# Sums of squares over all channels from a rounded pair instead of one float32 product, at three norms of a hybrid encoder layer

## Chip, core and metric

The kernel runs on one core of a Trainium2 chip. The metric is the device time of one execution in microseconds; the median of several runs counts. TensorE is called PE, VectorE DVE, ScalarE ACT, GpSimd POOL and SyncE SP, as in the profile.

## The reference

One streaming step of one layer, for 512 prompt frames and 64 sample frames (576 columns in the kernel), with 2048 channels:

```python
def rmsnorm(x, g):
    xf = x.astype(jnp.float32)
    y = xf * lax.rsqrt(jnp.mean(xf * xf, axis=-1, keepdims=True) + EPS) * g.astype(jnp.float32)
    return y.astype(x.dtype)

def hybrid_layer(x, ...):
    hn = rmsnorm(x, g_norm1)
    proj = hn @ w_in
    ...
    o_attn = stick_breaking_blocks(q, k_all, v_all, P).reshape(B, T, ATTN_W)
    ...
    o_conv = gb * conv
    mix = jnp.concatenate([rmsnorm(o_attn, g_attn_out), rmsnorm(o_conv, g_conv_out)], axis=-1)
    x = x + mix @ w_out
    h2 = rmsnorm(x, g_norm2)
    x = x + (jax.nn.silu(h2 @ w_gate) * (h2 @ w_up)) @ w_down
```

Four of its norms take a mean of squares over many channels. The change touches three: the one of the convolution's output (1024 channels), the one of the attention's output (1024) and the second norm of the layer (2048, `g_norm2`). The first norm of the layer and the norms of each head's queries and keys are as they were.

## The kernel before

**Layout.** Channels lie on the 128 partitions, frames on the free axis, in two halves of 288 columns (`HALVES`). Matmuls are done in rounded float32 (`F32R`), and each float32 operand is parted into a rounded part `hi` (a cast on ACT, L228) and the rest `lo` (a subtraction on DVE, L229), by `split`. A product is then three matmuls: hi*hi, lo*hi, hi*lo.

**Stages.** First the input projection, in units of weights (`HEADS_A`), each as seven products (`run`, `multiply`, L405) of sums of blocks of weights and inputs. Then the output projection in two passes (`out_proj`, L224): over the convolution's channels (`mixc`), with the attention of the eight heads running between its products, and over the attention's channels (`mixa`). Then the gate, up and down products of the feed-forward part, again as seven products per unit. Weights come by DMA to `raw_a` and `raw_b` (L328); sums of weight blocks are formed on DVE (L345, L349, L351, L353, with `s` a sum of blocks), and `prepare` parts a piece of weights into `whl` (128 x 1024, L228 and L229) four products ahead of its use. `psy`, `psx`, `psw` and `psv` are the PSUM banks of these products; `part` is a copy of psy (L428).

**The three norms.** The squares of the channels are added up elementwise as they are made: `accc` for the convolution, `accA` for the attention (both 128 x 576), `acc2` (two tiles of 128 x 288) for the second norm. What is left is the sum over the 128 partitions, which a matmul with a matrix of ones (`oner`) does and at once spreads to all partitions. In `group_scale` and `row_scale2` this is one plain float32 product per half (L866, L1416) into the bank `ssg` or `ss2`; then ACT and DVE form the inverse root: a scaled copy (L869, L1418), logarithm (L870, L1419), exponential (L871, L1420), square (L872, L1421), and two operations on DVE (L873 and L874, L1422 and L1423). The result stands in `accc` or `accA`, which scales the products of `out_proj` (L1110), or in `R2`, which scales the gate and up products (L1512). The norms of the heads (`normed`) already sum by `channel_sums`: two rounded matmuls (L283, L284) of parted squares; their parts `s2` are made by `a_done`, 12 to 24 ticks ahead.

**What sets the order.** PE's instructions run in the order in which the program is written. Work beside the products is in generators of a `Pipeline`: every group of three matmuls is a tick, and `yield n` puts a generator off by n ticks. `group_scale(accc[0], 3)` is spawned 13 ticks after a product of the input projection's last but one unit, `group_scale(accA, 2)` 9 ticks ahead of the second pass's place for it, and `row_scale2` waits 19 ticks into the feed-forward part. On ACT, DVE, POOL and SP a scheduler sets the order when the program is built; on the chip each engine then executes its queue in that order, and an instruction that waits holds what is behind it. Buffers of the pool `tmp` with the tag `hl` (128 x 2 x 288) go round between all users of the tag, three of them in the first stages and two from the second pass on.

The Silu of the gate (L1517) and the logarithm and exponential are in different function tables of ACT; a change between them is an `ACT_TABLE_LOAD`.

Of the kernel before, what the change touches and what calls it, by code (L numbers as in the profile page):

```python
# [10 lines left out]
F32 = mybir.dt.float32  # L11
F32R = mybir.dt.float32r
# [4 lines left out]
P = 128  # L17
# [3 lines left out]
HALF = T // 2  # L21
# [81 lines left out]
def tile_hybrid_stream_step(  # L103
# [7 lines left out]
    mm = nc.tensor.matmul  # L111
# [13 lines left out]
    tmp = tc.alloc_tile_pool(name="tmpa", bufs=2, side="left")  # L125
# [15 lines left out]
    def misc(name):  # L141
        return ps_z.tile([P, 512], F32, tag="misc", name=name, bufs=2)
# [75 lines left out]
    pipe = Pipeline()  # L218
# [8 lines left out]
    def split(hi, lo, src, lo_eng=None):  # L227
        cast = nc.scalar.copy(out=hi, in_=src)  # L228
        (lo_eng or nc.vector).tensor_tensor(out=lo, in0=src, in1=hi.bitcast(F32), op=ALU.subtract)  # L229
        return cast.ins  # L230
# [8 lines left out]
    oner = const.tile([P, P], F32R, name="oner")  # L239
# [41 lines left out]
    def channel_sums(src_hi, src_lo, a, b, name):  # L281
        ps = misc(name)[:, : b - a]
        mm(ps, oner, src_hi, start=True, stop=False)  # L283
        mm(ps, oner, src_lo, start=False, stop=True)  # L284
        return ps
# [576 lines left out]

    def group_scale(acc_, bufs):
        for a, b in HALVES:
            ss = misc("ssg")[:, :HALF]
            mm(ss, oner.bitcast(F32), acc_[:, a:b], start=True, stop=True)  # L866
            yt = tmp.tile([P, 2, HALF], F32, tag="hl", name="ytg", bufs=bufs)
            y, t = yt[:, 0], yt[:, 1]
            nc.scalar.activation(out=ss, in_=ss, func=AF.Identity, scale=1.0 / (8 * P), bias=epsc)  # L869
            nc.scalar.activation(out=y, in_=ss, func=AF.Ln)  # L870
            nc.scalar.activation(out=y, in_=y, func=AF.Exp, scale=-0.5)  # L871
            nc.scalar.activation(out=t, in_=y, func=AF.Square)  # L872
            nc.vector.scalar_tensor_tensor(out=t, in0=t, scalar=-0.5, in1=ss, op0=ALU.mult, op1=ALU.mult)  # L873
            nc.vector.scalar_tensor_tensor(out=acc_[:, a:b], in0=t, scalar=1.5, in1=y, op0=ALU.add, op1=ALU.mult)  # L874
            yield 1
# [118 lines left out]
    for k_, (n, p_) in enumerate(order):  # L994
        run(n, p_, n in early)
        if k_ + 4 < len(order):
            prepare(*order[k_ + 4])
            if order[k_ + 4] in ((-2, 3), (-1, 6)):
                load_weight()
        if (n, p_) == (-2, 6):  # L1000
            pipe.spawn(group_scale(accc[0], 3), 13)
        if (n, p_) == (-1, 3):
            xpool.release()
            cpool = tc.alloc_tile_pool(name="cpool", bufs=1, reuse_waits="tile", side="right")
            mixc = cpool.tile([P, NG, 2, T], F32R, name="mixc")
            for g in range(NG):
                nc.sync.dma_start(out=mixc[:, g].bitcast(F32), in_=mixc_dram[g])
        if (n, p_) == (-1, 5):
            split_weight(nc.vector)
        if (n, p_) == (-1, 7):  # L1010
            first = next_weight(), ps_pj.tile([P, HALF], F32, tag="pj", name="pjo")
            product(first[1], *first[0], slice(0, P), mixed_conv, 8, 0, HALF)
# [307 lines left out]
    accA = bt["accA"]  # L1320
# [3 lines left out]
    tmp = tc.alloc_tile_pool(name="tmp", bufs=2, reuse_waits="tile", side="left")  # L1324
    lpad = tc.alloc_tile_pool(name="lpad", bufs=1, side="left")
    lpad.tile([P, 64], F32, name="lpad_t")
    pipe.spawn(group_scale(accA, 2), 9)

# [14 lines left out]
    acc2 = [apool.tile([P, HALF], F32, name=f"acc2_{i}") for i in range(2)]  # L1345
# [66 lines left out]
    def row_scale2():  # L1412
        yield 19
        for i, (a, b) in enumerate(HALVES):
            ss = misc("ss2")[:, :HALF]
            mm(ss, oner.bitcast(F32), acc2[i], start=True, stop=True)  # L1416
            y, t = (tmp.tile([P, HALF], F32, tag=tag, name="y2") for tag in ("y", "r"))
            nc.scalar.activation(out=ss, in_=ss, func=AF.Identity, scale=1.0 / D, bias=epsc)  # L1418
            nc.scalar.activation(out=y, in_=ss, func=AF.Ln)  # L1419
            nc.scalar.activation(out=y, in_=y, func=AF.Exp, scale=-0.5)  # L1420
            nc.scalar.activation(out=t, in_=y, func=AF.Square)  # L1421
            nc.vector.scalar_tensor_tensor(out=t, in0=t, scalar=-0.5, in1=ss, op0=ALU.mult, op1=ALU.mult)  # L1422
            nc.vector.scalar_tensor_tensor(out=R2[:, a:b], in0=t, scalar=1.5, in1=y, op0=ALU.add, op1=ALU.mult)  # L1423
        apool.release()

    pipe.spawn(row_scale2())
    tpool.release()

# [311 lines left out]
```

## Time and profile before

| | |
|---|---|
| median of 3 runs | 2326.66 us (2326.58 to 2326.91) |
| the profiled execution: time | 2327.18 us |
| its span in the profile | 2325.5 us |
| PE busy | 2315.3 us |
| DVE, ACT, POOL busy | 1951.5, 1222.1, 304.3 us |
| sums of accc, accA, acc2 on PE | at 538.6, 752.6 and 859.7 us |

Times in views are microseconds from the span's start. In rows of the timeline stand the start, the duration, the engine, the line, the operation, output<-inputs, the shape, and the number of instructions taken together; in brackets the idle time of the engine ahead of it and what ended that. PE's matmuls are pipelined: one of 288 columns has a duration of 0.29 us, while the next starts 0.13 us after it. PEld is the load of a stationary operand, beside the matmuls. The Ls are line numbers of the kernel before.

### The profile page before, as it was taken

How to read it: one execution, taken by the hardware profiler on the slowest of the kernel's cores; microseconds unless marked ns; L12 is line 12 of the kernel's file. 1: busy time of each engine (PE TensorE's matmuls, PEld its weight loads, DVE VectorE, ACT ScalarE, POOL GpSimd, SP SyncE). 2: the span in 40 equal slices, each digit the busy share in tenths (PEclk: the TensorE clock that was granted, in tenths of full speed). 3: DMA queues.
4: the chain of work that ended last, by engine and by line, in shares of the span. 5: the costliest groups of instructions: out<-in, count | busy, mean ns of one | idle time of the engine just before them, and what ended most of it. 6: DMA issues, size and time to landing. Idle time of an engine off the chain costs nothing.

```text
span 2325.5 us, 43556 instructions
## 1 busy us (share of the span) xinstructions
PE 2315.3 (100%) x17432; PEld 2306.9 (99%) x17432; DVE 1951.5 (84%) x2871; ACT 1222.1 (53%) x2170; POOL 304.3 (13%) x374
## 2 busy tenths in 40 slices
PE   9999999999999999999999999999999999999999
PEld 9999999999999999999999999999999999999999
DVE  8898989897777898888888888888888777987897
ACT  8566656456887564444444444444444444444443
POOL 0212121110432320000000000000000002431222
PEclk9999999999999999999999999999999999999999
DMA  8444343546653554544444444344344936885654
GB/s 273 136 118 130 91 142 107 147 129 209 191 148 101 173 200 128 155 138 141 149 135 150 131 148 155 112 157 157 117 155 134 351 129 205 228 240 184 209 128 108
DMA packets 533674, 368.57 MB, mean 158 GB/s; under 512 B 70246, under 2 KB 517888, under 8 KB 533472
## 3 DMA queue, kind: packets, MB, share of 16 engines
q1 hardware_dynamic: 526976, 356.42, 48.8%
q0 software_dynamic: 6384, 9.24, 2.3%
q8 instruction: 136, 2.23, 0.4%
q14 instruction: 66, 0.54, 0.1%
q10 hardware_dynamic: 112, 0.14, 0.0%
HBM read 285.52 MB, written 80.23 MB: 157 GB/s over the span
## 4 chain that ended last, share of the span: by engine, by line
PE 94%; ACT 3%; DVE 2%; POOL 1%; issue 0%; DMA 0%; SPq 0%; POOLq 0%; ACTq 0%; DVEq 0%
PE psy L405 47%; PE psw L405 24%; PE psx L405 12%; PE pjo L224 6%; PE pj L691 1%; PE pjz L691 1%; PE psv L405 1%; PE pjm L691 1%; ACT ph L228 0%; PE psx L556 0%; DVE pr L1134 0%; DVE wlo L177 0%; POOL pr L1189 0%; ACT whi L176 0%; DMA vtok<-v_dram 0%
## 5 line engine op out<-in xcount | busy, mean ns | idle before, releaser
L229 DVE TENSOR_TENSOR whl<-raw_a,whl 128x1024 fp32r<-128x1024 f32 (+4 forms) x384 | 429.8, 1120 | 55.5 <-ACT whl L228 54.1
L405 PE MATMUL psy<-t,whl 128*128 128x288 f32 x3000 | 447.0, 294 | 0.0
L228 ACT CAST whl<-raw_a 128x1024 fp32r<-128x1024 f32 (+4 forms) x384 | 360.1, 940 | 140.0 <-PE psx L405 44.9
L405 PE MATMUL psy<-h_s,whl 128*128 128x288 f32 x2766 | 416.6, 294 | 0.0
L405 PEld LDWEIGHTS psy<-t,whl 128*128 128x128 f32 x3000 | 414.4, 188 | 0.0
L405 PE MATMUL psw<-t,whl 128*128 128x288 f32 x2688 | 388.9, 294 | 0.0
L405 PEld LDWEIGHTS psy<-h_s,whl 128*128 128x128 f32 x2766 | 383.1, 188 | 0.2
L405 PEld LDWEIGHTS psw<-t,whl 128*128 128x128 f32 x2688 | 366.8, 188 | 0.0
L228 ACT CAST whl<-raw_b 128x1024 fp32r<-128x1024 f32 (+5 forms) x234 | 211.4, 905 | 208.2 <-issue 71.4
L229 DVE TENSOR_TENSOR whl<-raw_b,whl 128x1024 fp32r<-128x1024 f32 (+5 forms) x234 | 256.1, 1095 | 73.4 <-ACT whl L228 72.4
L428 ACT COPY part<-psy 128x288 f32<-128x288 f32 x309 | 123.2, 399 | 347.9 <-PE psy L405 345.5
L405 PE MATMUL psx<-h_s,whl 128*128 128x288 f32 x1164 | 170.2, 294 | 0.0
L228 ACT CAST whl<-s 128x1024 fp32r<-128x1024 f32 (+5 forms) x103 | 95.3, 925 | 124.3 <-PE psw L405 116.4
L405 PEld LDWEIGHTS psx<-h_s,whl 128*128 128x128 f32 x1164 | 159.6, 188 | 0.0
L405 PE MATMUL psw<-t34a,whl 128*128 128x288 f32 x1056 | 150.4, 295 | 0.0
L405 PE MATMUL psy<-t12a,whl 128*128 128x288 f32 x1056 | 150.4, 295 | 0.0
L405 PEld LDWEIGHTS psw<-t34a,whl 128*128 128x128 f32 x1056 | 143.5, 188 | 0.0
L405 PEld LDWEIGHTS psy<-t12a,whl 128*128 128x128 f32 x1056 | 143.3, 188 | 0.2
L1455 POOL DMA_DIRECT2D hid_dram<-form x7 | 5.2, 736 | 951.6 <-DVE form L229 944.5
L229 DVE TENSOR_TENSOR whl<-s,whl 128x1024 fp32r<-128x1024 f32 (+5 forms) x103 | 110.3, 1071 | 20.3 <-ACT whl L228 19.6
L224 PE MATMUL pjo<-mixc,whi 128*128 128x288 f32 x512 | 118.7, 299 | 0.0
L224 PE MATMUL pjo<-mixa,whi 128*128 128x288 f32 x512 | 102.8, 295 | 0.0
(565 smaller groups left out, 3922.0 us busy)
## 6 DMA issues: line engine op xcount, KB each, us to landing
hid_dram<-form SPq DMA_DIRECT2D x147, 288.0 KB
raw_a<-in_w_in_dram SPq DMA_DIRECT2D x22, 1024.0 KB
raw_b<-in_w_in_dram SPq DMA_DIRECT2D x22, 1024.0 KB
raw_b<-in_w_gate_dram SPq DMA_DIRECT2D x22, 1024.0 KB
raw_b<-in_w_up_dram SPq DMA_DIRECT2D x22, 1024.0 KB
raw_a<-in_w_gate_dram SPq DMA_DIRECT2D x22, 1024.0 KB
raw_a<-in_w_up_dram SPq DMA_DIRECT2D x22, 1024.0 KB
h_s<-hid_dram SPq DMA_DIRECT2D x10, 2016.0 KB
```

Source lines behind the costliest of these rows:

```text
L224: mm(ps, w_[:, k, csl], x_[:, a:b], start=(k == 0 and n == 0), stop=(k == nk - 1 and n == 2))
L228: cast = nc.scalar.copy(out=hi, in_=src)
L229: (lo_eng or nc.vector).tensor_tensor(out=lo, in0=src, in1=hi.bitcast(F32), op=ALU.subtract)
L405: mm(ps, whl[:, w_, j, :], x_, start=(start and j == 0 and q == 0), stop=(j == len(xs_) - 1 and q == 2), skip_group_check=True)
L428: nc.scalar.copy(out=t, in_=st["y"])
L691: mm(banks_[c][i], w3[:, kt % 8, c * P : (c + 1) * P], t[:, x_, :], start=(kt == 0 and n == 0), stop=(kt == KD - 1 and n == 2))
L1455: q.dma_start(out=hid_dram[fp][2 * n - 2 : 2 * n].rearrange("f p t -> p f t"), in_=t.bitcast(F32))
```

## The change

At all three norms each half of the sum of squares is first parted by `split` into a new tile (`s2g`, `s2r`), with a cast on ACT and a subtraction on DVE. Three ticks later (two in `row_scale2`) `channel_sums`, which was there for the heads, multiplies both parts by the ones, as two rounded matmuls into one bank. In `group_scale` the second half's split comes only after the first half's sums; the spawn for `accA` is three ticks earlier in exchange.

```diff
     def group_scale(acc_, bufs):
         for a, b in HALVES:
-            ss = misc("ssg")[:, :HALF]
-            mm(ss, oner.bitcast(F32), acc_[:, a:b], start=True, stop=True)
+            s2 = tmp.tile([P, 2, HALF], F32R, tag="hl", name="s2g", bufs=bufs)
+            split(s2[:, 0], s2[:, 1], acc_[:, a:b])
+            yield 3
+            ss = channel_sums(s2[:, 0], s2[:, 1], a, b, "ssg")
             yt = tmp.tile([P, 2, HALF], F32, tag="hl", name="ytg", bufs=bufs)
...
-    pipe.spawn(group_scale(accA, 2), 9)
+    pipe.spawn(group_scale(accA, 2), 6)
...
     def row_scale2():
         yield 19
         for i, (a, b) in enumerate(HALVES):
-            ss = misc("ss2")[:, :HALF]
-            mm(ss, oner.bitcast(F32), acc2[i], start=True, stop=True)
+            s2 = tmp.tile([P, 2, HALF], F32R, tag="hl", name="s2r", bufs=2)
+            split(s2[:, 0], s2[:, 1], acc2[i])
+            yield 2
+            ss = channel_sums(s2[:, 0], s2[:, 1], a, b, "ss2")
```

What it calls, unchanged:

```python
    def split(hi, lo, src, lo_eng=None):
        cast = nc.scalar.copy(out=hi, in_=src)
        (lo_eng or nc.vector).tensor_tensor(out=lo, in0=src, in1=hi.bitcast(F32), op=ALU.subtract)
        return cast.ins

    def channel_sums(src_hi, src_lo, a, b, name):
        ps = misc(name)[:, : b - a]
        mm(ps, oner, src_hi, start=True, stop=False)
        mm(ps, oner, src_lo, start=False, stop=True)
        return ps
```

In the changed kernel the lines behind the first edit have numbers two higher (L871 is L869 of before), those behind the last four higher. On PE, POOL and SP the rest of the order is the same, but for two neighbouring DMAs on SP that change places. On PE the sums stand later: at place 1 (accc) the first pair comes three groups of three psy matmuls later, at the end of that product, and the second after twelve matmuls of the following psx product; at place 2 (accA) the first pair has the slot of the first float32 product, the second comes 12 matmuls behind it, where before there were three; at place 3 (acc2) the first pair comes after 18 matmuls of a psy product instead of 12, the second six matmuls later, where before both products stood together.

Place 1, DVE's queue at the convolution's norm, before (`yt` and `E` belong to a head's norm, `ytg` to this one):

```order
L353 TENSOR_TENSOR raw_a<-raw_a 128x8x128
L853 SCALAR_TENSOR_TENSOR yt<-yt,ss 128x288
L854 SCALAR_TENSOR_TENSOR yt<-yt 128x288
L855 SCALAR_TENSOR_TENSOR E_6158<-E_6158,gqs,yt 128x288
L229 TENSOR_TENSOR whl<-raw_a,whl 128x1024
L873 SCALAR_TENSOR_TENSOR ytg<-ytg,ssg 128x288
L874 SCALAR_TENSOR_TENSOR accc<-ytg 128x288
L229 TENSOR_TENSOR whl<-raw_b,whl 128x1024
L873 SCALAR_TENSOR_TENSOR ytg<-ytg,ssg 128x288
```

and now:

```order
L353 TENSOR_TENSOR raw_a<-raw_a 128x8x128
L229 TENSOR_TENSOR s2g<-accc,s2g 128x288
L853 SCALAR_TENSOR_TENSOR yt<-yt,ss 128x288
L854 SCALAR_TENSOR_TENSOR yt<-yt 128x288
L229 TENSOR_TENSOR whl<-raw_a,whl 128x1024
L855 SCALAR_TENSOR_TENSOR E_6158<-E_6158,gqs,yt 128x288
L229 TENSOR_TENSOR whl<-raw_b,whl 128x1024
L229 TENSOR_TENSOR s2g<-accc,s2g 128x288
L875 SCALAR_TENSOR_TENSOR ytg<-ytg,ssg 128x288
L876 SCALAR_TENSOR_TENSOR accc<-ytg 128x288
```

The first subtraction stands behind L353, the second behind the parting of a piece of raw_b. On ACT the second cast stands, in this order, behind a copy of psy (L428), the scaled copy of the first half (L869 of before), the cast of that piece of raw_b, and the first half's logarithm (L870).

Place 2, DVE's queue at the attention's norm, before (`wlo` are parts of the output projection's weights, `s` a sum of the first feed-forward weights):

```order
L177 TENSOR_TENSOR wlo_8787<-raw_a,whi_8786 128x512 x4
L345 TENSOR_TENSOR s_10011<-raw_b 128x1024
L873 SCALAR_TENSOR_TENSOR ytg<-ytg,ssg 128x288
L874 SCALAR_TENSOR_TENSOR accA<-ytg 128x288
L1110 TENSOR_TENSOR pjo<-pjo,accA 128x288
```

and now:

```order
L177 TENSOR_TENSOR wlo_8795<-raw_a,whi_8794 128x512 x2
L229 TENSOR_TENSOR s2g<-accA,s2g 128x288
L177 TENSOR_TENSOR wlo_8795<-raw_a,whi_8794 128x512 x2
L345 TENSOR_TENSOR s_10027<-raw_b 128x1024
L875 SCALAR_TENSOR_TENSOR ytg<-ytg,ssg 128x288
L229 TENSOR_TENSOR s2g<-accA,s2g 128x288
L876 SCALAR_TENSOR_TENSOR accA<-ytg 128x288
L1112 TENSOR_TENSOR pjo<-pjo,accA 128x288
```

The first subtraction stands amid the four wlo, the second behind the sum of raw_b (L345) and the first half's own L873.

Place 3, DVE's queue at the second norm, before (`t12z` and `t_7` are parts of the last input blocks):

```order
L229 TENSOR_TENSOR whl<-raw_a,whl 128x1024
L229 TENSOR_TENSOR t12z<-ta,t12z 128x288 x2
L229 TENSOR_TENSOR whl<-raw_a,whl 128x1024
L229 TENSOR_TENSOR t_7_10159<-tb,t_7_10159 128x288 x2
L1422 SCALAR_TENSOR_TENSOR y_10192<-y_10192,ss_10189 128x288
```

and now:

```order
L229 TENSOR_TENSOR whl<-raw_a,whl 128x1024
L229 TENSOR_TENSOR t12z<-ta,t12z 128x288 x2
L229 TENSOR_TENSOR s2r<-acc_0_8790,s2r 128x288
L229 TENSOR_TENSOR s2r<-acc_1_8791,s2r 128x288
L229 TENSOR_TENSOR whl<-raw_a,whl 128x1024
```

Both subtractions stand between those of t12z and the next piece of weights. Behind them ACT's queue at the same place, before:

```order
L228 CAST whl<-raw_b 128x1024
L1421 ACTIVATE y_10202<-y_10201 128x288
L428 COPY part<-psy 128x288
L228 CAST whl<-s_10011 128x1024
L1517 ACT_TABLE_LOAD
L1517 ACTIVATE gs<-gs 128x288
```

and now:

```order
L228 CAST whl<-raw_b 128x1024
L1423 ACTIVATE y_10241<-ss_10238 128x288
L1521 ACT_TABLE_LOAD
L1521 ACTIVATE gs<-gs 128x288
L1424 ACT_TABLE_LOAD
L1424 ACTIVATE y_10241<-y_10241 128x288
L228 CAST whl<-s_10027 128x1024
L1425 ACTIVATE y_10242<-y_10241 128x288
```

The first Silu (L1517, now L1521) has come between the second half's logarithm and its exponential, with a table load on either side, and the cast of whl from s stands behind them; a third load stands ahead of the following Silu.

## Prediction

> **What bounds the kernel now.** I read the page first (busy times, the granted clock by slices, the chain that ended last), then the view of TensorE's (PE's) waits (total, times, longest).
>
> ```profile
> span 2325.5 us, 43556 instructions
> PE 2315.3 (100%) x17432; PEld 2306.9 (99%) x17432; DVE 1951.5 (84%) x2871; ACT 1222.1 (53%) x2170; POOL 304.3 (13%) x374
> PEclk9999999999999999999999999999999999999999
> PE 94%; ACT 3%; DVE 2%; POOL 1%; issue 0%; DMA 0%; SPq 0%; POOLq 0%; ACTq 0%; DVEq 0%
> PE psx L556 <- DMA xin<-in_x_prompt_dram: 4.0, 1, 4.0
> PE zs L1298 <- ACT ws L1225: 1.0, 3, 0.6
> ```
>
> PE works for 2315.3 of 2325.5 us and is 94% of the chain. Its largest wait is 4.0 us ahead of the first load; the next is 1.0 us in all. It executes in order and has no idle time later in which a delay could vanish: a microsecond taken from PE's work is gained, and a microsecond for which PE waits for ACT or DVE is lost, one for one. So the question is what six sums cost on PE, and whether their operands are there when PE comes to them.
>
> **The saving on PE.** Two rounded matmuls take the place of one float32 product, six times. Rows of the timeline (start, duration, engine):
>
> ```profile
> 535.09 0.29 PE L283 MATMUL ss<-s,oner 128*128 128x288 f32 x1
> 535.22 0.30 PE L284 MATMUL ss<-s,oner 128*128 128x288 f32 x1
> 535.35 1.38 PE L405 MATMUL psy<-b,whl 128*128 128x288 f32 x9
> 538.56 0.65 PE L866 MATMUL ssg<-accc,oner 128*128 128x288 f32 x2
> 540.72 3.33 PE L405 MATMUL psx<-bod,whl 128*128 128x288 f32 x24
> 543.89 3.33 PE L405 MATMUL psy<-bod,whl 128*128 128x288 f32 x24
> 547.07 3.33 PE L405 MATMUL psv<-bod,whl 128*128 128x288 f32 x24
> ```
>
> The pair that the heads' norms already use occupies PE from 535.09 to 535.35: 0.26 us. One rounded matmul is (547.07 - 543.89) / 24 = 0.1325. From 538.56 to 540.72 stand two float32 products and nine matmuls: 2.16 - 1.19 = 0.97, or 0.485 each. At the third norm (rows below) it is (862.28 - 858.10) - 24 x 0.1325 = 1.00, or 0.50. With 0.49, the change saves 0.49 - 0.265 = 0.225 us six times: **-1.35 us**.
>
> **What it adds** is, per half of a norm, a 288-wide cast on ACT (0.42 us, the t12z row below) and a 288-wide subtraction on DVE (0.45), queued in program order. PE's second matmul waits for the subtraction. Their busy time lies beside PE's; where they stand in the queue decides.
>
> **Place 1, the convolution's norm.**
>
> ```profile
> 536.12 0.41 ACT L850 ACTIVATE yt<-ss 128x288 f32<-128x288 f32 x1
> 536.95 1.21 DVE L353 TENSOR_TENSOR raw_a<-raw_a 128x1024 f32<-128x1024 f32 x1
> 540.54 0.46 ACT L869 ACTIVATE ssg<-ssg,epsc 128x288 f32<-128x288 f32 x1
> 540.92 0.43 ACT L872 ACTIVATE ytg<-ytg 128x288 f32<-128x288 f32 x1
> 542.17 1.05 ACT L228 CAST whl<-raw_b 128x1024 fp32r<-128x1024 f32 x1
> 543.26 1.22 DVE L229 TENSOR_TENSOR whl<-raw_b,whl 128x1024 fp32r<-128x1024 f32 x1 [0.85 <-ACT whl L228]
> ```
>
> On PE the first pair now follows nine more psy matmuls: 538.56 + 1.19 = 539.75. Its cast stands right behind L850, its subtraction behind L353 (538.08 to 538.53): in time, no wait. The second pair is due 0.26 + 12 x 0.1325 later, at 541.59 and 541.72. Its cast stands behind the copy of psy (from 539.94, when the nine end), L869's activation (540.24), the raw_b cast (540.24 + 0.38 = 540.60), and L870 (0.95 later, 541.55); it runs from 541.88. Its subtraction stands behind the raw_b subtraction, which starts 1.09 after its cast: 541.69. A 1024-wide one holds DVE for 1.13 (860.50 to 861.63 below), so it runs 542.82 to 543.27, and PE, 0.05 later, at 543.32. Wait: 543.32 - 541.72 = **1.6 us**.
>
> **Place 2, the attention's norm.**
>
> ```profile
> 750.50 1.16 ACT L176 CAST whi<-raw_a 128x512 fp32r<-128x512 f32 x2
> 751.05 2.49 DVE L177 TENSOR_TENSOR wlo<-raw_a,whi 128x512 fp32r<-128x512 f32 x4
> 752.55 0.65 PE L866 MATMUL ssg<-accA,oner 128*128 128x288 f32 x2
> 754.82 1.23 DVE L345 TENSOR_TENSOR s<-raw_b 128x1024 f32<-128x1024 f32 x1 [1.28 <-DMA raw_b<-in_w_gate_dram]
> 755.96 0.45 DVE L873 SCALAR_TENSOR_TENSOR ytg<-ytg,ssg 128x288 f32<-128x288 f32 x1
> ```
>
> The first pair keeps its slot, 752.55. Its subtraction follows two of the four wlo (0.62 each): 752.29 to 752.74, PE at 752.79 instead of 752.68: 0.1 us. The second pair is due 12 matmuls later, at 754.50 and 754.63. But its subtraction now stands behind L345, which waits for a weight load that lands at 754.82, and behind L873: 755.96 + 0.37 = 756.33 to 756.82, PE at 756.87. Wait: **2.25 us**. The load does not depend on PE here, so nothing moves it up.
>
> **Place 3, the second norm of the layer.**
>
> ```profile
> 858.10 1.75 PE L405 MATMUL psy<-h_s,whl 128*128 128x288 f32 x12
> 862.28 0.56 PE L405 MATMUL psv<-h_z,whl 128*128 128x288 f32 x3
> 858.00 0.42 ACT L228 CAST t12z<-ta 128x288 fp32r<-128x288 f32 x1
> 860.09 1.05 ACT L228 CAST whl<-raw_a 128x1024 fp32r<-128x1024 f32 x1
> 861.04 0.46 ACT L1418 ACTIVATE ss<-ss,epsc 128x288 f32<-128x288 f32 x1
> 860.50 1.21 DVE L229 TENSOR_TENSOR whl<-raw_a,whl 128x1024 fp32r<-128x1024 f32 x1
> 861.63 0.82 DVE L229 TENSOR_TENSOR t12z<-ta,t12z 128x288 fp32r<-128x288 f32 x2
> 862.37 1.21 DVE L229 TENSOR_TENSOR whl<-raw_a,whl 128x1024 fp32r<-128x1024 f32 x1
> ```
>
> The first pair comes after 18 psy matmuls: 858.10 + 2.39 = 860.49, its second matmul 860.62. Its subtraction takes the slot at 862.37, behind the whl and both t12z ones: done 862.82, PE at 862.87: **2.25 us**. The second half's is done 0.37 later, PE comes six matmuls later: no wait.
>
> **What is late next.** Behind place 3 ACT gets two more table loads, and the second half's exponential stands between them:
>
> ```profile
> 866.41 1.05 ACT L228 CAST whl<-s 128x1024 fp32r<-128x1024 f32 x1
> 867.48 1.28 ACT L1517 ACT_TABLE_LOAD   x1
> 870.74 1.23 DVE L349 TENSOR_TENSOR raw_b<-raw_b,raw_a 128x1024 f32<-128x1024 f32 x1
> 878.15 3.33 PE L405 MATMUL psw<-t,whl 128*128 128x288 f32 x24
> 881.32 0.56 PE L405 MATMUL psv<-h_z,whl 128*128 128x288 f32 x3
> ```
>
> L1418 waits for the first sum and starts near 863.2 instead of 861.04. From there ACT has eight 288-wide steps of 0.33 to 0.55 (3.1 us) and the raw_b cast (0.95), to 867.3; then L1419, a load, the Silu, a load and the exponential (0.35 + 1.28 + 0.35 + 1.28 + 0.45): the whl<-s cast moves from 866.41 to 871.0. DVE, idle until then, does the whl<-s subtraction (from 872.1), L345 and the two small steps of R2 and comes to L349 near 875.1, 4.4 us later than before. What hides this is PE's store of prepared weights. The psw at 878.15 takes an operand that is cast behind L349 and ready at 875.1 + 1.25 + 1.1 + 1.2 = 878.7; PE, itself 1.9 late here, comes at 880.0. The psv at 881.32 takes one that stands three 1024-wide and two small DVE steps behind the start of that subtraction: 877.5 + 3 x 1.13 + 2 x 0.37 + 1.22 = 882.8; PE's first matmul that needs it comes at 883.3. The cover is 0.5 us, so I cost the delay at nothing. Were the cover gone, each microsecond would cost one; the bounds are 0 and 1.3 (one table load).
>
> **Restart.** After a wait the next matmuls come slower:
>
> ```profile
> 747.88 1.00 PE L1298 MATMUL zs<-ws,cV 128*128 128x64 f32 x8
> 709.83 0.42 ACT L1225 ACTIVATE ws<-zs 128x320 f32<-128x320 f32 x1
> 710.30 1.10 PE L1298 MATMUL zs<-ws,cV 128*128 128x64 f32 x8 [0.62 <-ACT ws L1225]
> ```
>
> The operand was done at 710.25, PE went on at 710.30 (the 0.05 used above), and eight matmuls took 1.10 instead of 1.00: 0.1 per wait, between 0 and 0.13 (a full matmul step). Five of the twelve matmuls wait (at place 1 also that of the second cast, done 542.3, due 541.59; at place 2 those of both subtractions; at place 3 one): 0.5 us.
>
> **Sum.** 1.6 + 0.1 + 2.25 + 2.25 + 0.5 - 1.35 = **+5.35 us**. The profiled run took 2327.18 us (its span, 2325.5, and 1.7 around it), so 2332.5; the median shown is 0.52 lower, 2326.66, so **2332.0 us**, +0.23%. 0.2% (4.65 us, 2331.3) is about what a measurement of this kernel can tell from no change; the forecast lies just beyond.
>
> **Rivals.** (a) *The operands come in time* (not slower): at the heads' 32 pairs PE never waits for the same split, with 20 ticks between split and sum; here it has 2 or 3. It decides if the subtractions end by 541.7, 754.6 and 860.6. Against it stands the DVE queue at all three places. Then only the saving is left: 2326.66 - 1.35 = 2325.3. 6%.
> (b) *Some waits are shorter*: if at place 2 the load lands by 753.9, when DVE is free, L873 is held by its own chain until about 755.4 and the wait falls to 1.7; at place 1 the cast chain has four links of 0.3 to 0.4, each of which may be shorter. Taking 1.5 to 2 us off: 2330.3. 20%.
> (c) *The cover behind place 3 is gone*: one or two table loads reach PE, +1.3 to +2.6: 2334. 14%.
> (d) *PE's clock falls in the waits.* The granted clock is 9 tenths or more in all slices, also in the first with its 4.0 us wait; but no row shows a wait of 2 us in mid-run. At half rate for some 3 us behind each place: +1.5 three times, 2336.5. 3%. The Trainium skill (TensorE: Matmul & The Clock Gate, Part 1: The HAM clock gate) has the clock halved after an idle window of about 3.4 us; by it waits of at most 2.3 us cost nothing more, and the sum stays.
> (e) *The pair is no cheaper* (0.49 for two): no saving, 2333.4. 1%.
>
> **How the numbers follow.** The forecast has 56%, its own range 2331 to 2333.5 (restarts 0 to 0.65, each wait right to some 0.3). Slower by over 0.2%: nine tenths of it, (c), (d), (e): 0.68. Within: its rest, (b) and most of (a): 0.30. Faster by that much would need a gain three times the saving: 0.02. Range 2329.0 to 2335.0: it takes in (b) and (c).
>
> **What would show it.** PE waits at L283 and L284 <- DVE s2g and s2r: about 1.6, 2.3 and 2.3 us, near 542, 755 and 862; pairs of 0.26; L345 still held by the raw_b load until after 754; two more table loads by 872; no wait on whl near 883. I am wrong if the waits come to under 4 us, or if PE waits for whl behind place 3.

## Result and profile after

The changed kernel took 2334.07 us, the median of 8 executions (2332.45 to 2335.91); the kernel before, run beside it, 2327.40 us (2326.58 to 2328.67, 8 executions). The ratio is 1.0027, with a 95% interval of 1.0018 to 1.0036: slower by 6.7 us. The forecast was 2332.0, with a range of 2329.0 to 2335.0, and slower as the likeliest. The profiled execution took 2333.75 us, with a span of 2332.1, 6.6 more than before.

First the page of the changed kernel (span, busy time, granted clock by slices, chain that ended last), then its view of PE's waits (total, times, longest):

```profile
span 2332.1 us, 43568 instructions
PE 2316.4 (99%) x17432; PEld 2307.4 (99%) x17432; DVE 1953.5 (84%) x2877; ACT 1226.1 (53%) x2178; POOL 303.8 (13%) x374
PEclk9999999999999999999999999999999999999999
PE 87%; DVE 6%; ACT 4%; issue 1%; DMA 1%; POOL 1%; SPq 0%; POOLq 0%; DVEq 0%; ACTq 0%
```

```profile
PE ssg L284 <- DVE s2g L229: 2.3, 2, 1.7
PE ss L284 <- DVE s2r L229: 1.9, 1, 1.9
PE ssg L283 <- ACT s2g L228: 0.6, 1, 0.6
PE ss L283 <- ACT s2r L228: 0.3, 1, 0.3
```

PE is still busy nearly all the time. Its share of the chain fell from 94% to 87%, since the chain, followed back from the end, now leaves PE at a new wait and goes on along DVE and ACT for a while; that share is no measure of time lost. The four new waits are all at the new sums, 5.1 us in all. No wait for `whl` stands behind the third place.

The timeline of PE in the changed kernel at the three places (start, duration; in brackets the idle time and what ended it):

```profile
539.86 1.78 PE L405 MATMUL psx<-bod,whl 128*128 128x288 f32 x12
542.22 0.40 PE L283 MATMUL ssg<-s2g,oner 128*128 128x288 f32 x1 [0.58 <-ACT s2g L228]
543.22 0.40 PE L284 MATMUL ssg<-s2g,oner 128*128 128x288 f32 x1 [0.60 <-DVE s2g L229]
543.45 1.77 PE L405 MATMUL psx<-bod,whl 128*128 128x288 f32 x12
...
753.42 0.29 PE L283 MATMUL ssg<-s2g,oner 128*128 128x288 f32 x1
753.87 0.29 PE L224 MATMUL pjo<-mixa,whi 128*128 128x288 f32 x1
755.46 0.30 PE L283 MATMUL ssg<-s2g,oner 128*128 128x288 f32 x1
757.46 0.40 PE L284 MATMUL ssg<-s2g,oner 128*128 128x288 f32 x1 [1.70 <-DVE s2g L229]
757.70 0.29 PE L224 MATMUL pjo<-mixa,whi 128*128 128x288 f32 x1
...
860.68 2.53 PE L405 MATMUL psy<-h_s,whl 128*128 128x288 f32 x18
863.50 0.40 PE L283 MATMUL ss<-s2r,oner 128*128 128x288 f32 x1 [0.28 <-ACT s2r L228]
865.80 0.55 PE L284 MATMUL ss<-s2r,oner 128*128 128x288 f32 x1 [1.90 <-DVE s2r L229]
866.15 0.92 PE L405 MATMUL psy<-h_s,whl 128*128 128x288 f32 x3
878.15 3.33 PE L405 MATMUL psw<-t,whl 128*128 128x288 f32 x24
```

At the first place the matmuls go on at the usual pace, twelve in 1.6 us, and at the second too. Behind the third they do not: three matmuls have a duration of 0.92 us where the kernel before has 0.56, and start 0.24 us apart instead of 0.13. The view of windows (length, busy time of each engine, granted clock, DMA) of the changed kernel, in steps of 3.41 us around that point, says why:

```profile
862.48:865.89 3.41, 1.22 (x8) 0.78 (x6) 3.41 (x8) 2.16 (x5) 0.00 (x0) 1.00 0.32 122
865.89:869.30 3.41, 3.41 (x15) 3.41 (x16) 2.68 (x6) 2.87 (x8) 0.00 (x0) 0.50 1.07 305
869.30:872.71 3.41, 3.41 (x27) 3.41 (x27) 2.38 (x4) 3.36 (x6) 0.00 (x0) 1.00 0.99 365
```

For 3.41 us PE had half its clock: 15 matmuls instead of 27. The slices of the page cannot show it, since one of them is 58 us long: they show a 9 throughout, as before.

**Where the 6.6 us went.** The starts of the same rows in both timelines, after minus before:

| ahead of and behind | shift ahead | shift behind | the place costs |
|---|---|---|---|
| place 1 (psy at 535.35, psy at 543.89 before) | -0.14 | +1.17 | 1.31 |
| place 2 (sum at 752.55, psy at 858.10) | +0.87 | +2.58 | 1.71 |
| place 3 (psy at 858.10, psw at 871.80) | +2.58 | +6.35 | 3.77 |

Together 6.8; the start, the stretch between the first two places and the end make up -0.2.

### The profile page after: what moved, and what is told of

The parts are those of the page before. It is cut to its first block, busy times and chain, and to the rows that moved or that the text cites. A ratio compares the mean times of both kernels' runs of the same rounds, so it can differ in the third digit from the quotient of the medians.

```text
span 2332.1 us, 43568 instructions
## 1 busy us (share of the span) xinstructions
PE 2316.4 (99%) x17432; PEld 2307.4 (99%) x17432; DVE 1953.5 (84%) x2877; ACT 1226.1 (53%) x2178; POOL 303.8 (13%) x374
## 4 chain that ended last, share of the span: by engine, by line
PE 87%; DVE 6%; ACT 4%; issue 1%; DMA 1%; POOL 1%; SPq 0%; POOLq 0%; DVEq 0%; ACTq 0%
PE psy L405 47%; PE psw L405 24%; PE psx L405 12%; PE pjo L224 1%; DVE wlo L177 1%; PE psv L405 1%; PE pjz L691 1%; PE pjm L691 1%; DVE pjo L1112 1%; DVE x L1113 0%; ACT ph L228 0%; DVE h_s L1386 0%; DVE pr L1136 0%; DMA xt_dram<-st 0%; ACT whi L176 0%
## 5 line engine op out<-in xcount | busy, mean ns | idle before, releaser
L428 ACT COPY part<-psy 128x288 f32<-128x288 f32 x309 | 123.0, 398 | 349.1 <-PE psy L405 345.5
```

Of the source, the lines that this page charges most:

```text
L428: nc.scalar.copy(out=t, in_=st["y"])
```

## The experiments

The theory: each place costs the wait for its own subtraction, less the 0.45 us that two pairs save, and the third also loses 1.5 us because PE idles long enough there for its clock to fall. "The place costs" is from here on read as in the table above, from the shift of the same rows in one profiled execution; the medians scatter by about 1 us, and each interval of a ratio is 0.0009 to either side (2.1 us).

### One place at a time

`e1_place1` and `e2_place2` keep the changed lines of `group_scale` for one accumulator, and `e3_place3` those of `row_scale2`; the rest is as in the kernel before. Shown is the first; in `e2_place2` the condition is `bufs == 2`, and the spawn for `accA` is 6 ticks ahead as in the change:

```diff
         for a, b in HALVES:
+            if bufs == 3:
+                s2 = tmp.tile([P, 2, HALF], F32R, tag="hl", name="s2g", bufs=bufs)
+                split(s2[:, 0], s2[:, 1], acc_[:, a:b])
+                yield 3
+                ss = channel_sums(s2[:, 0], s2[:, 1], a, b, "ssg")
+            else:
+                ss = misc("ssg")[:, :HALF]
+                mm(ss, oner.bitcast(F32), acc_[:, a:b], start=True, stop=True)
```

> Only the convolution's norm uses the parted square; the other two norms keep the float32 product. Theory (each place pays its own wait for the subtraction, less 0.45 us saved by its two pairs; only the third also loses to a slower clock): two waits near 542 us, 0.6 and 0.6 us, full clock, kernel +1.3 us over the one before. Rival (the 6.6 us are one common loss, for example later weight stores or transfers, and do not divide by places): less than 0.5 or more than 2.5 us here. Rival (the pair is no cheaper): +1.7.

> Only the attention's norm uses the parted square. Theory: PE waits about 1.7 to 2.3 us at the second half's L284 (a little more than the 1.70 in the changed kernel, since PE arrives 0.9 us earlier there and the raw_b load that holds DVE may not follow), full clock after it, kernel +1.7 to +2.1 us. Rival (a wait of that length drops the clock by itself): half-rate matmuls behind 757 us and +3.3. Rival (one common loss): not between 1 and 2.5.

> Only the second norm of the layer uses the parted square. Theory: PE waits 0.3 us for the cast and 1.9 us for the subtraction near 862 us, the granted clock then falls to half for about 3 us, and the kernel is +3.8 us. Rival (the clock fell because waits of three places add up, or because of when the run came there): no slow stretch, +2.1 us. Rival (the two extra table loads on ACT cost PE something later): a PE wait for whl between 880 and 900 us and more than +3.8.

The second half's L284 in the timelines of `e1_place1` and `e2_place2`, the first half's in that of `e3_place3`, and the windows of `e3_place3` around it:

```profile
543.24 0.40 PE L284 MATMUL ssg<-s2g,oner 128*128 128x288 f32 x1 [0.60 <-DVE s2g L229]
```

```profile
756.74 0.40 PE L284 MATMUL ssg<-s2g,oner 128*128 128x288 f32 x1 [1.27 <-DVE s2g L229]
```

```profile
863.41 0.40 PE L284 MATMUL ss<-s2r,oner 128*128 128x288 f32 x1 [1.91 <-DVE s2r L229]
```

```profile
860.86:864.27 3.41, 1.26 (x7) 1.05 (x8) 3.41 (x7) 1.90 (x4) 0.00 (x0) 1.00 0.19 56
864.27:867.68 3.41, 3.41 (x16) 3.41 (x15) 2.79 (x7) 3.38 (x10) 0.00 (x0) 0.50 1.08 307
```

| | the place costs (profile) | median, and of the kernel before beside it | ratio and interval |
|---|---|---|---|
| place 1 alone | 1.32 | 2330.56, 2327.84 | 1.0007 (0.9998 to 1.0016) |
| place 2 alone | 1.29 | 2330.35, 2327.84 | 1.0007 (0.9998 to 1.0016) |
| place 3 alone | 3.95 | 2331.62, 2327.84 | 1.0014 (1.0005 to 1.0023) |

By the profiles the places stand alone and add up (6.56 against 6.79 in the changed kernel), and the third loses its clock without the other two: the rival by which the waits of several places add up falls. At place 2 the wait was shorter than expected, 1.27: the raw_b load was there when DVE came (L345 starts at 754.40 without a wait), and the subtraction was then held by the step of the first half ahead of it. The medians of the first two lie 2.7 and 2.5 us above the kernel before, 1.2 to 1.4 more than their places cost in the profile and more than the 1.3 and 1.7 to 2.1 that were expected. By its median alone place 1 would even lie where the rival of one common loss puts it (more than 2.5); it is the shift of the rows, which happens at the place, that speaks against this rival. The profiled executions were in the quicker half there (2329.62 and 2328.92), and what the others add is not shown. Losses of that size outside the places do stand in the profiles: in `e1_place1` PE waits 0.56 us at 1977 us for a copy on ACT (0.24 in `e3_place3`, none in the kernel before), and in `e2_place2` its waits for the first load come to 4.6 us instead of 4.0. That the three differences of medians add up to 9.0 where the whole change makes 6.7 is within their intervals.

### The halves parted together

`e4_parts_early` changes only the first two places, with the spawn as in the change, and parts both halves ahead of the first sum; `e11_parts_early_again` is the same kernel once more:

```diff
+        s2 = [tmp.tile([P, 2, HALF], F32R, tag="hl", name="s2g", bufs=bufs) for _ in HALVES]
+        for s_, (a, b) in zip(s2, HALVES):
+            split(s_[:, 0], s_[:, 1], acc_[:, a:b])
+        yield 3
+        for s_, (a, b) in zip(s2, HALVES):
+            ss = channel_sums(s_[:, 0], s_[:, 1], a, b, "ssg")
...
-            yield 1
+            yield 4
```

> The convolution's and the attention's norm use the parted square, but both halves are parted before the first sum, so that the second half's subtraction stands ahead of the raw_b work in DVE's queue; the layer's second norm keeps the float32 product. Theory (queue position alone makes the waits): at most 0.1 us of waiting at L284 in all, the two pairs per place 0.26 us each, kernel -0.8 us against the one before (four products saved at 0.225 us, less 0.1). Rival (the pair is no cheaper): 0. Rival (the added casts and subtractions themselves, 4 x 0.4 us on ACT and DVE, delay PE's operands wherever they stand): +0.5 or more.

> The same kernel as e4_parts_early (first two norms with both halves parted ahead of the first sum, third norm with the float32 product), run again because its first interval reached from -2.8 to +1.4 us. Theory: -0.8 us against the kernel before, the medians of all its runs below those of before by 0.5 to 1. Rival (no gain): the two medians agree.

Rows of the timeline of PE and DVE in `e4_parts_early`:

```profile
539.85 0.29 PE L283 MATMUL ssg<-s2g,oner 128*128 128x288 f32 x1
540.11 1.78 PE L405 MATMUL psx<-bod,whl 128*128 128x288 f32 x12
751.54 0.82 DVE L229 TENSOR_TENSOR s2g<-accA,s2g 128x288 fp32r<-128x288 f32 x2
754.01 0.29 PE L284 MATMUL ssg<-s2g,oner 128*128 128x288 f32 x1
```

No new wait is left in PE's list. Both subtractions for `accA` now stand together on DVE, ahead of L345 and of the load that held the second. A pair takes 540.11 - 539.85 = 0.26 us, and place 1 now gains 0.42 us and place 2 0.26: the pair is as cheap as priced, and the casts and subtractions cost nothing where they are in time. The medians were 2327.15 against 2327.84 and, in the second series, 2327.27 against 2328.11, 0.7 and 0.8 us lower as expected; both ratios are 0.9997 with an interval of 0.9988 to 1.0006, so a gain of this size is likely but not shown by the times alone.

### The subtractions of place 3 on POOL

`e5_p3_pool` is `e3_place3` with `split(s2[:, 0], s2[:, 1], acc2[i], nc.gpsimd)`; `e8_all` joins that with the first two places of `e4_parts_early`.

> Only the layer's second norm uses the parted square, as in e3_place3, but its two subtractions run on GpSimd (POOL), which is idle there, instead of behind the whl and t12z ones on DVE. Theory (DVE's queue makes the wait, and the clock falls only when PE idles for most of a 3.4 us stretch): POOL takes about 0.8 us for 288 columns (its L1393 rows: 0.80 to 1.43), so PE waits 0.4 us for the cast and 0.8 to 1.5 us at the first L284; idle 1.2 to 2 us, full clock behind it; kernel +0.8 to +1.6 us over the one before, that is 2 to 3 us below e3_place3. Rival (the clock falls after this place for a reason of its own, such as its dense transfers): half-rate matmuls again, +2.5 or more. Rival (POOL is slowed by DVE's traffic to several us): wait above 2 us and half rate.

> All three norms use the parted square; at the first two both halves are parted ahead of the first sum (e4_parts_early), at the third the subtractions run on POOL (e5_p3_pool). Theory: -0.8 from the first two places and +0.8 to +1.6 at the third, full clock: within 1 us of the kernel before, 6 us below the changed kernel. Rival (the places do not add): anything above +2.

Rows of the timeline of `e5_p3_pool` and one of its windows; then, for it and for `e8_all`, the line of the view of the tile s2r with POOL's two subtractions (least, median and longest time in ns, first and last start), and a row of DVE's timeline in `e8_all`:

```profile
860.99 4.40 POOL L229 TENSOR_TENSOR s2r<-acc,s2r 128x288 fp32r<-128x288 f32 x2 [1.56 <-DVE tb L1367]
864.69 0.40 PE L284 MATMUL ss<-s2r,oner 128*128 128x288 f32 x1 [3.32 <-POOL s2r L229]
```

```profile
865.23:868.64 3.41, 3.41 (x16) 3.41 (x16) 1.64 (x4) 3.38 (x9) 0.16 (x1) 0.50 1.05 325
```

```profile
L229 POOL TENSOR_TENSOR s2r<-acc,s2r x2: 795/2218/3641, 861.0 to 864.6; 128x288 fp32r<-128x288 f32 x2
```

```profile
L229 POOL TENSOR_TENSOR s2r<-acc,s2r x2: 1021/1393/1765, 861.5 to 863.2; 128x288 fp32r<-128x288 f32 x2
```

```profile
862.49 2.02 DVE L229 TENSOR_TENSOR t12z<-ta,t12z 128x288 fp32r<-128x288 f32 x2
```

This went the way of the last rival. The same subtraction takes POOL 0.80 us or 3.64, according to what DVE does beside it: in `e5_p3_pool` the first one began at 860.99, within a run of `whl` and t12z subtractions on DVE, and ended at 864.63, 0.65 us behind the run's end at 863.98; and in `e8_all`, where it lasted 1.77, DVE's two t12z steps took 2.02 us instead of 0.81. The Trainium skill (SBUF — State Buffer, section "SBUF: two separate sides") says that a GpSimd instruction that reads SBUF and a DVE one with two inputs there lock each other out of a shared pair of ports for a whole instruction; the rows agree, and show the loss on either side. With a wait of 3.3 us and the half clock behind it the third place cost 4.85 us here, and the kernel 2333.63 against 2327.88 (1.0024, 1.0014 to 1.0033). `e8_all` came to 2331.78 against 2327.88 (1.0015, 1.0006 to 1.0024), not within 1 us: its profiled execution was one in which POOL was quick and the clock stayed full (2330.33), but in 7 of its 11 executions the mean granted clock was below 1.000.

### A longer wait at place 2

Is it the place or the idle time that takes the clock? `e6_p2_wait1` and `e7_p2_wait2` are `e2_place2` with the second half's subtraction done once more (`1` below) or twice (`2`):

```diff
                 split(s2[:, 0], s2[:, 1], acc_[:, a:b])
+                for _ in range(1 if a else 0):
+                    nc.vector.tensor_tensor(out=s2[:, 1], in0=acc_[:, a:b], in1=s2[:, 0].bitcast(F32), op=ALU.subtract)
```

> As e2_place2 (only the attention's norm), but the second half's subtraction is done twice, the same result written again, so that PE's wait there grows by 0.75 to 0.85 us (the repeat and the L876-type step that goes ahead of it). Theory (the clock gate looks at fixed stretches of 3.41 us that run on by themselves, and halves the clock for one stretch when PE was idle for most of the last): idle about 2.2 us in one piece; whether it trips depends on how the stretch falls, so about half of the executions show a clock of 0.999 (2 of 11 did with 1.4 us idle, 17 of 19 with 2.6 us at the third norm), and those are about 1.7 us longer; median +1.6 over e2_place2 or so. Rival (only the third norm's place loses clock): every execution at 1.000, +0.8 over e2_place2. Rival (an idle piece must be 3.4 us): the same, none.

> As e6_p2_wait1 with the second half's subtraction done three times; PE's wait grows by about 1.6 us over e2_place2, idle about 3 us in one piece. Theory: nearly all executions show 0.999 and a stretch of 3.41 us at half rate right behind 757 us; kernel +3.3 us over e2_place2 (1.6 of wait, 1.7 of clock). Rivals (place 3 only, or 3.4 us of idle needed): full clock, +1.6 over e2_place2.

Two rows of PE's timeline and then the windows of `e6_p2_wait1`:

```profile
754.33 0.29 PE L283 MATMUL ssg<-s2g,oner 128*128 128x288 f32 x1
757.39 0.61 PE L284 MATMUL ssg<-s2g,oner 128*128 128x288 f32 x1 [2.77 <-DVE s2g L869]
```

```profile
753.33:756.74 3.41, 1.30 (x10) 1.08 (x8) 2.41 (x5) 1.60 (x5) 0.00 (x0) 1.00 1.02 283
756.74:760.15 3.41, 2.76 (x11) 2.76 (x12) 1.95 (x5) 2.08 (x6) 0.00 (x0) 0.50 0.70 247
760.15:763.56 3.41, 3.41 (x16) 3.41 (x15) 2.35 (x5) 1.53 (x4) 0.00 (x0) 0.50 0.00 0
763.56:766.97 3.41, 3.41 (x27) 3.41 (x27) 1.74 (x4) 0.87 (x2) 0.07 (x1) 1.00 0.00 0
```

It is the idle time. At place 2, where the clock had stayed full, it now falls, and the rival of the place is out. So is the rival that the piece of idle time must be 3.4 us: from the end of the matmul at 754.33, which takes 0.13 us, to 757.39 it is 2.9 us. The clock fell at 756.74, while PE was still waiting, so it does not follow the end of the wait. It stayed at half for two stretches of 3.41 us, and the first of these had 0.65 us of idle time in it. The wait itself had grown by more than planned, since the raw_b load held L345 again.

Times: 2332.11 and 2332.77 against 2327.88 (1.0017, 1.0009 to 1.0026, and 1.0021, 1.0012 to 1.0029). Against the kernel before beside each, that is 1.7 and 2.4 us more than `e2_place2`; 1.6 and 3.3 were expected. The mean granted clock was below 1.000 in 8 of 11 executions of `e6_p2_wait1` and in all 11 of `e7_p2_wait2`, against 2 of 11 with the plain wait (`e2_place2`), 10 of 11 of `e3_place3` and 7 of 8 of the changed kernel; of the kernel before it was so in 7 of 105. About half was expected at the first step, nearly all at the second. A mean below 1.000 is not always a lost stretch behind a wait, for the clock also falls when the matmuls have ended: in the changed kernel at 2330.21, 1.9 us before the span's end, in `e5_p3_pool` 2.3 us before it. A mean that rounds to 0.999 needs some 2.3 us at half rate (an estimate: 0.0005 of 2330 us, twice), so the end alone can just make it; whether it did in those 7 is not shown.

### The idle time of place 3 filled

`e9_p3_filled` is `e3_place3`, and `e10_filled` the whole change, with 12 matmuls that PE repeats while it would wait at the third place; the pair behind them overwrites what they leave. `fill` is 12 for the first half in `row_scale2`, and 0 everywhere else.

```diff
-    def channel_sums(src_hi, src_lo, a, b, name):
+    def channel_sums(src_hi, src_lo, a, b, name, fill=0):
         ps = misc(name)[:, : b - a]
+        for _ in range(fill):
+            mm(ps, oner, src_hi, start=True, stop=True)
```

> As e3_place3 (only the layer's second norm uses the parted square, subtractions on DVE), but ahead of the first half's pair stand 12 more matmuls with the same operands as its first one, whose results the pair overwrites: 1.6 us of work inside the 2.2 us in which PE waits for the subtraction anyway. Theory (the half-rate stretch comes from PE being idle for most of a 3.41 us stretch, and is a loss of its own beside the wait): the wait at L284 shrinks from 1.9 to about 0.4 us, the pair ends when it did, the clock stays full, and the kernel is 1.7 us below e3_place3, +2.1 over the one before; all executions at 1.000. Rival (the slow stretch belongs to the operands' way or the traffic there, not to PE's idleness): half rate as before, no gain.

> The whole change (all three norms) with the same 12 extra matmuls at the layer's second norm. Theory: no half-rate stretch at the third place, 1.7 us below the changed kernel: about +5.0 over the one before, 2332.4. Rival (the clock is lost elsewhere instead, or the fill delays what follows): as the changed kernel, +6.6, or more.

Rows of PE's timeline in `e9_p3_filled`, and one of its windows:

```profile
862.26 1.85 PE L284 MATMUL ss<-s2r,oner 128*128 128x288 f32 x12
864.56 0.40 PE L286 MATMUL ss<-s2r,oner 128*128 128x288 f32 x1 [0.32 <-DVE s2r L229]
864.80 0.55 PE L407 MATMUL psy<-h_s,whl 128*128 128x288 f32 x3
875.38 3.33 PE L407 MATMUL psw<-t,whl 128*128 128x288 f32 x24
```

```profile
864.56:867.97 3.41, 3.41 (x25) 3.41 (x26) 3.41 (x6) 3.25 (x8) 0.00 (x0) 1.00 1.04 309
```

The pair still waits for the same subtraction, but the clock stays full: the place costs 2.03 us instead of 3.95, and 11 of 11 executions had a mean clock of 1.000. The kernel took 2329.44 against 2328.11 (1.0006, 0.9997 to 1.0015), 1.3 us above the kernel before, where `e3_place3` was 3.8 above it; the two intervals overlap, so it is the rows and the clock that show the gain. So the lost clock is a loss of its own beside the wait, of 1.9 us by these two costs, of 1.4 by the pace of the rows (below).

`e10_filled` was expected 1.7 us below the changed kernel, and came to 2333.93 against 2328.11 (1.0026, 1.0017 to 1.0036): no gain in the median. In its profiled execution place 3 costs 2.07 us, as it should, but now place 2 has lost its clock (a row of PE's timeline, and two windows):

```profile
758.09 0.52 PE L286 MATMUL ssg<-s2g,oner 128*128 128x288 f32 x1 [2.02 <-DVE s2g L229]
```

```profile
754.80:758.21 3.41, 1.39 (x11) 1.18 (x10) 2.42 (x5) 1.58 (x5) 0.00 (x0) 1.00 1.01 288
758.21:761.62 3.41, 3.41 (x15) 3.41 (x16) 2.20 (x6) 2.85 (x7) 0.00 (x0) 0.50 0.66 235
```

The wait there was 2.02 us in that execution, against 1.70 in the changed kernel's. The executions divide: in five the mean clock was 1.000 and the mean time 2333.1, in four it was below and the mean 2335.5. Against the kernel before beside them the five are 5.0 us slower, which is what was expected without the lost clock.

### Both remedies

`e12_early_filled` is the whole change with the first two places as in `e4_parts_early` and the third as in `e9_p3_filled`.

> All three norms use the parted square: the first two with both halves parted ahead of the first sum (e4_parts_early), the third on DVE with the 12 extra matmuls inside its wait (e9_p3_filled). Theory (two waits removed by queue position, the third left at its length but without the lost clock): no idle piece of PE above 0.6 us at the three places, clock 1.000 in all executions, -0.8 and about +1.7 (what e9_p3_filled came to against the before of its runs, 1.3, and in its trace, 2.1): +0.9 over the kernel before, about 2329. Rival (the clock or the waits return in another place, as in e10_filled): above +2.5.

It took 2329.02 (2328.40 to 2329.93) against 2328.23, 0.8 us slower (1.0005, 0.9996 to 1.0014), where 0.9 was expected. The mean clock was 1.000 in 9 of 11 executions, not in all as expected; the other two (2328.84 and 2329.93) have no profile. The only new wait in the profiled execution's list is

```profile
PE ss L286 <- DVE s2r L229: 0.3, 1, 0.3
```

About 5.9 of the 6.7 us are thus taken back by two things: another place of the subtractions in DVE's queue at the first two norms, and no idle PE at the third. No version with all three places was found that beats the kernel before; the one that likely does, by less than a microsecond, leaves the third norm's float32 product in place.

## Why the prediction was right, and by how much it was off

**The saving** (1.35 us) is confirmed: pairs of 0.26 us, and gains of 0.42 and 0.26 us at the two places of `e4_parts_early`, where nearly nothing waits.

**The waits and restarts** were priced at 6.7 us together. From the rows: at place 1 PE should have reached the second pair at 541.45 and left it at 541.72, and went on at 543.45, 1.74 us lost (priced 1.6 and two restarts of 0.1). At place 2 it lost 753.87 - 753.42 - 0.26 = 0.19 at the first pair and 757.70 - 755.46 - 0.26 = 1.98 at the second, together 2.17 (priced 2.35 and two restarts). At place 3 the eighteen psy end at 863.07 and the next start at 866.15, 0.26 of which is the pair: 2.82 lost (priced 2.25 and one restart). Sum 6.73. The mechanism, the engine and the row that ends each wait were as forecast. At place 1 the second subtraction ran from 542.71, behind the raw_b one that started at 541.57, where 542.82 and 541.69 were forecast. Rows of DVE in the changed kernel at the other two places:

```profile
755.45 1.23 DVE L345 TENSOR_TENSOR s<-raw_b 128x1024 f32<-128x1024 f32 x1 [0.67 <-DMA raw_b<-in_w_gate_dram]
756.95 0.45 DVE L229 TENSOR_TENSOR s2g<-accA,s2g 128x288 fp32r<-128x288 f32 x1
865.30 0.81 DVE L229 TENSOR_TENSOR s2r<-acc,s2r 128x288 fp32r<-128x288 f32 x2
```

That the sum fits so closely is partly luck, for two sizes were off against each other. Counted as in the prediction, from when a pair's second matmul was due to its start, place 2 waited 1.87 us (757.46 - 755.59) instead of 2.25: PE came there 0.96 us later than forecast, since the forecast counted from the timeline of before and left out what place 1 adds, while L345 started only 0.63 later. Place 3 waited 2.60 (865.80 - 863.20) instead of 2.25: DVE came to its queue there 0.34 us later against PE than before (`whl` at 863.42 and psy at 860.68, before 860.50 and 858.10). A restart cost about 0.1 us, as priced: behind a wait the next matmul starts 0.23 or 0.24 us later instead of 0.13 (543.22 to 543.45, 757.46 to 757.70). The 0.28 us for which PE waits for the cast at place 3, which I had left out, cost nothing more, since the same pair waits for the subtraction until later.

**Place 2** was held by the raw_b load in the changed kernel, as said. But the load does not keep its time: in `e2_place2` it came earlier and the wait was 1.27, which is rival (b).

**What was missed is PE's clock.** Rival (d) had the right price, half rate for some 3 us or 1.5 us a place, but I gave it 3% and all three places. It happened at one, in nearly every execution: from 866.15 to 878.15 the changed kernel needs 12.0 us for what takes `e9_p3_filled` 10.6 (864.80 to 875.38), 1.4 us. With it the sum is 6.73 - 1.35 + 1.42 - 0.2 = 6.6 us, the span's difference. Of the 2.1 us by which the median lies above the forecast, 1.3 come from this; the other 0.7 are the kernel before, which took 2327.40 beside it instead of 2326.66. The step that failed is the argument for the 3%: the granted clock's slices, "9 tenths or more in all", are 17 times longer than the stretch in question, and the first wait of 4.0 us, which I took for evidence, stands ahead of the first matmul of all. It speaks rather for the contrary: in the timeline of the kernel before two matmuls soon behind it start 0.24 us apart,

```profile
7.18 0.44 PE L691 MATMUL pj<-b,wlo 128*128 128x288 f32 x1
7.42 0.52 PE L691 MATMUL pj<-b,whi 128*128 128x288 f32 x1
```

the pace of half rate, although the windows give a clock of 1.00 there. The trace has no entry for the clock ahead of 10.80 us; full clock is entered from there on, and at 11.35 and 11.48 matmuls start 0.13 us apart. So most likely PE ran at half clock up to then, and the 1.00 ahead of it only says that nothing was recorded.

The other leg was the page that I cited. By the Trainium skill (TensorE: Matmul & The Clock Gate, Part 1: The HAM clock gate) the clock is halved after an idle window of 3.4 us that runs on freely. Its length and its free running agree with the traces: each stretch at half rate lasts 3.41 us or twice that, and they begin 0.1 us behind the waiting matmul's start in the changed kernel, 0.9 behind in `e3_place3`, 0.65 ahead in `e6_p2_wait1`. From the drop at place 3 of the changed kernel (865.89) to the one behind its last matmuls (2330.21) it is 1464.32 us, 429 times 3.4133; from the drop at place 2 of `e10_filled` (758.21) to that at its end it is 1573.55, 461 times 3.4133. But the window need not be idle: the ones ahead of the drops at the places had PE busy for 1.22, 1.26, 1.30, 1.39 and 1.40 of 3.41 us (the changed kernel, `e3_place3`, `e6_p2_wait1`, `e10_filled`, `e7_p2_wait2`), and for 0.54 in `e5_p3_pool`. So waits of 2 us can cost the clock, and I concluded from the page that they cannot.

**Behind place 3** the table loads came and the whl casts were late, and PE did not wait for them: (c) did not happen, and the cost of nothing was right, though PE's own lateness of 6.35 us instead of 1.9 gave the casts more room than I had counted on.

**Rivals (a) and (e)** did not happen. What (a) needed, the subtractions in time, is what `e4_parts_early` makes.

## What to carry to other kernels

When an operand of an in-order engine is given one more step on another engine, what counts is what stands ahead of that step in the other engine's queue, not its own length: issued one loop turn earlier, the same 0.4 us step costs nothing. A wait of PE of around 2 us costs more than its length when most of it falls into one window of the clock gate; look at the granted clock in windows of a few microseconds there, for coarse slices hide it. If such a wait cannot be avoided, fill it, even with matmuls whose result is thrown away; two pieces within one window can cost the clock as well (`e3_place3` waited 0.43 and 1.91 us).

## What was not expected of the hardware

- The clock gate, which grants PE's clock, decides by fixed windows of 3.41 us, wherever a wait begins. Since the clock also falls at the end of each program, the windows can be counted back from there, and so be placed where the clock did not fall:

| run | window | PE busy in it | clock behind it |
|---|---|---|---|
| `e10_filled`, place 2 | 754.80 to 758.21 | 1.39 | half |
| `e7_p2_wait2`, place 2 | 753.13 to 756.54 | 1.40 | half |
| `e12_early_filled`, the end | 2320.64 to 2324.05 | 1.71 | full |
| `e2_place2`, place 2 | 753.80 to 757.22 | 2.15 | full |
| the changed kernel, place 2 | 753.25 to 756.66 | 2.51 | full |
| the changed kernel, place 2 | 756.66 to 760.07 | 2.61 | full |

  In the changed kernel a border of two windows fell into the wait of 1.70 us at place 2, and neither half was idle enough; that is why it kept its clock there. In these traces the bound lies between 1.40 and 1.71 us of 3.41 (by PE's busy time in the profile, whose ends are modelled).
- Because the phase of the windows is not tied to the program, the same kernel shows the drop in some executions only: by the mean clock 2 of 11 with a wait of 1.27 us in the profiled one (`e2_place2`), 10 of 11 with 0.4 and 1.91 (`e3_place3`), 8 of 11 with 2.77 (`e6_p2_wait1`) and 11 of 11 with 3.3 (`e7_p2_wait2`).
- A window at half rate with 0.65 us of idle time in it is followed by a second one at half rate; a full one was enough in the others.
- A 288-column subtraction on POOL takes from 0.80 to 3.64 us beside DVE's two-input subtractions, and slows these from 0.81 to 2.02 us for two.
